# A modulation matrix applied on VectorE, ScalarE and GpSimd instead of on TensorE, in a two-layer hybrid mixer

## The chip, the cores and the metric

The kernel runs on one core of one Trainium2 chip. The metric is the device time of one execution in microseconds; the kernel before has a median of 1401.21 us in three runs. The profile is of one execution.

## The reference

Two layers are applied to a prompt (128 tokens) and to a sample (512 tokens), with a model width of 1024, and both with the same weights. A layer mixes three branches: latent attention (A), differential attention (B) and a gated linear recurrence, mLSTM (C). What matters here is the modulation at a layer's head:

```python
mod = silu(c) @ W_mod[l] + b_mod[l]            # for the sample; silu(c_ctx) for the prompt
shift, scale, gate = jnp.split(mod, 3, axis=-1)
h = rmsnorm(x, g_norm[l]) * (1 + scale) + shift
proj = h @ W_in[l]                              # 1024 x 5840, split into the branches' inputs
...                                             # branches A, B and C
y = concat([o_a * silu(z_a), o_b * silu(z_b), o_c * silu(z_c)]) @ W_out[l]
x_new = x + gate * y
```

`W_mod` is 2 x 1024 x 3072 in fp32, so a layer's `mod` is two vectors (sample and prompt) times a 1024 x 3072 matrix. All is fp32.

## The kernel before

All 640 tokens are worked on together: four tiles of 128 sample tokens and one tile of the prompt. An exact fp32 product is made of three fp32r matmuls (`mm3`, L287 to L290): each operand is split into a high part, rounded to fp32r, and the rest. For weights `load_w` (L266 to L285) does this in pieces of at most 128 x 1088 values: SyncE's queue loads a piece into one of three raw slots (L278), ScalarE casts it to the high part (L279), and VectorE, or for every third piece GpSimd, subtracts to get the low part (L282).

Work that waits on nothing but `hT`, the normalised input, is written as units that a `Feed` hands out. A dependent chain (the gates, four mLSTM heads, four heads of differential attention, the latent branch) yields a number of microseconds after each step, and `Feed.pull` emits units, portion by portion, until as much has been yielded by them. The order of the units of a layer is the string `ORDER` (L133). On top of that the framework's scheduler orders the instructions of each engine, so that a cast or a load may stand earlier than in the program. `feed.need` forces units to be finished before a chain goes on.

`W_mod` is used in units of 256 columns, 24 in all:
- Eight units (the shift and scale of layer 0) are computed at the start, when there is no other work for TensorE, unsplit. The change leaves them as they are.
- Four *gate units* per layer (`gt0` to `gt3`, `mod_gate`) make 256 columns of the residual gate each, for the same layer.
- Eight *column units* (`mod0` to `mod7`, `mod_col`), in layer 0 only, make the shift and scale of layer 1.

The last sixteen go through `mod_rows` with `pool=3`: `load_w` loads and splits two pieces of 4 x 256 columns, and sixteen matmuls with four stationary columns (the two vectors, high and low) accumulate over the 1024 rows:

```python
hv, lv = load_w([(wmod[l, :, :, c0:c0 + 256], 0, 256)], 8, 256, pool)
for k in range(8):
    T.matmul(ps[0:4, 0:256], lhsT=cst4[:, k, :], rhs=hv[k], start=(k == 0), stop=False)     # L329
    T.matmul(ps[0:4, 0:256], lhsT=cst4[:, k, :], rhs=lv[k], start=False, stop=(k == 7))     # L330
```

ScalarE copies the four rows out of PSUM (L332). A column unit then turns them into columns with two small matmuls (L344) against a constant that adds the high and the low row, and VectorE adds the bias (L347). A gate unit adds the high and low rows with one matmul (L367), adds the bias (L370) and stores two rows to `grow` in DRAM, from which `gate_tile` later loads them on all partitions for the out-projection.

Other places that the prediction's steps touch: L615 and L616 are multiply-adds of the short convolution on VectorE; L756 and L759 are products and sums of the mLSTM heads on VectorE and GpSimd; L781 is the last product of an mLSTM head; L797 is the sum of the rotary embedding on GpSimd; L990 is the first norm of the latent branch, which starts after the last head of differential attention. Tiles called `fix` and `fixr` are cut from two big ones, so many names in the trace are the same; `qt` takes one of 35 slots, `pj` one of two PSUM buffers.

Of the kernel before, what the change touches and what calls it, by code (L numbers as in the profile page):

```python
# [13 lines left out]
ALU = mybir.AluOpType  # L14
# [51 lines left out]
def parameter_columns(I):  # L66
    """Vectors of the inputs laid out as columns of 128, and the gate biases and stabilisers on their gate rows."""
# [12 lines left out]
class Feed:  # L80
    """Independent work, emitted in portions between the steps of a dependent chain."""
# [41 lines left out]
def tile_hybrid(ctx: ExitStack, tc: tile.TileContext, I: dict, O: dict):  # L123
# [8 lines left out]
    # independent work of a layer, in the order in which it fills the gaps of the dependent chains  # L132
    ORDER = ("va0 qk0 mo0 zc0 qk1 gt0 zc1 qk2 gt1 va1 mo1 zc2 "  # L133
             "gt2 qk3 zc3 lam0 dv0 gt3 dqk0 mod0 mod1 zb0 dqk1 mod2 "
             "zb1 dv1 dqk2 mod3 mod4 zb2 dqk3 mod5 c0 zb3 c1 c2 "
             "za1 za0 mod6 za2 mod7 za3")
# [3 lines left out]
    class Fixed:  # L140
        """One tile from which all that stays in its place is cut."""
# [14 lines left out]
    class Ring:  # L156
        """Slots used in turn, for tiles that live for a short stretch of the program."""
# [32 lines left out]
    # ---------------------------------------------------------------- constants and parameters  # L190
# [12 lines left out]
    # silu(cond) as stationary columns: [c_hi, ctx_hi, c_lo, ctx_lo] per k  # L203
# [5 lines left out]
    cst4 = fixr.tile([P, 8, 4])  # L209
    cv3 = cth.rearrange("p (w k) -> p k w", w=2)  # L210
# [6 lines left out]
    # half conv weights; norm gains with the half of z's silu  # L217
# [45 lines left out]
    def load_w(parts, kt, w, pool=3):  # L263
        """Streams a weight section; returns per-k views of its exact high and low parts."""
# [27 lines left out]
    # ---------------------------------------------------------------- modulation  # L292
# [4 lines left out]
    def mod_rows(l, c0, pool):  # L297
        ps = pj("modp")
        if pool is None:
            # before there is other work for the tensor engine: unsplit  # L300
# [25 lines left out]
        else:  # L326
            hv, lv = load_w([(wmod[l, :, :, c0:c0 + 256], 0, 256)], 8, 256, pool)
            for k in range(8):
                T.matmul(ps[0:4, 0:256], lhsT=cst4[:, k, :], rhs=hv[k], start=(k == 0), stop=False)  # L329
                T.matmul(ps[0:4, 0:256], lhsT=cst4[:, k, :], rhs=lv[k], start=False, stop=(k == 7))  # L330
# [4 lines left out]
    def mod_col(l, part, s, res, pool=3):  # L335
        """Columns [P, k, which] of two feature tiles of the shift or of the scale."""
# [3 lines left out]
        mr = mod_rows(l, part * 1024 + s * 256, pool)  # L340
        yield 2.5
        ps = sm("mcp")
        for i in range(2):
            T.matmul(ps[:, 2 * i:2 * i + 2], lhsT=mr[0:4, i * P:(i + 1) * P],  # L344
                     rhs=con[0:4, C_SEL:C_SEL + 2], start=True, stop=True)
# [4 lines left out]
    def mod_end(l, res, k=slice(0, 8)):  # L350
        """(1 + scale) * g and shift."""
# [11 lines left out]
    def mod_gate(l, s, pool=3):  # L363
        mr = mod_rows(l, 2048 + s * 256, pool)
        yield 2
        ps = sm("gtp")
        T.matmul(ps[0:2, 0:256], lhsT=con[0:4, C_SEL:C_SEL + 2], rhs=mr[0:4, :], start=True, stop=True)  # L367
# [860 lines left out]
    def mod_col_(part, s):  # L1228
        for _ in mod_col(0, part, s, R, None):
            pass  # L1230
# [134 lines left out]
```

## Time and profile before

| | |
|---|---|
| median of 3 runs | 1401.21 us (1399.54 to 1405.23) |
| the profiled execution | span 1399.6 us, no time listed beside it |
| TensorE busy | 1310.0 us (94%), mean granted clock 0.977 |
| VectorE, ScalarE, GpSimd busy | 842.5, 630.2, 385.5 us |
| changed units in the trace | 16, from 130.7 to 949 us |

Engines are named PE (TensorE matmuls), PEld (its weight loads), DVE (VectorE), ACT (ScalarE), POOL (GpSimd) and SP (SyncE, here only a queue of loads). An fp32 matmul shows as two records. Matmuls are pipelined: the duration of one record is longer than its distance to the next, so what a matmul occupies is read from the chain or from start to start. The chain that ended last is followed back from the last instruction to what released each step.

### The profile page before, as it was taken

The page shows a single profiled execution, that of the slowest core. Times are in us where ns is not written, and L with a number is a line of the kernel's source. Part 1 is how long each engine was busy: PE and PEld are TensorE (multiplying, and loading weights), DVE is VectorE, ACT ScalarE, POOL GpSimd, SP SyncE. Part 2 cuts the span into 40 slices and gives each one's busy share as a digit, 9 for nine tenths or more (in the row PEclk, how much of TensorE's full clock was granted, in tenths as well). Part 3 has the DMA queues.
Part 4 walks back from the last instruction along what each step waited for, and adds up shares of the span by engine and source line. Part 5 has one row for each costly group of instructions (what it writes and reads, how often), then busy time and mean ns, then how long its engine had stood idle before and what let it go on. Part 6 is the DMA issues. An engine that isn't in the chain of part 4 may idle for free.

```text
span 1399.6 us, 24039 instructions
## 1 busy us (share of the span) xinstructions
PE 1310.0 (94%) x9300; PEld 1218.9 (87%) x9300; DVE 842.5 (60%) x1786; ACT 630.2 (45%) x1333; POOL 385.5 (28%) x335
## 2 busy tenths in 40 slices
PE   8989999989899999999979899999999999899995
PEld 3789899969899999798769899998799999878984
DVE  2576757765567465854465767675655646385446
ACT  5454544433455545255365345443343445435433
POOL 0421422323223013511432213333322202161142
PEclk9999999999999999999989999999999999999998
DMA  9423323264223223531751333434521211242154
GB/s 341 116 83 101 111 84 112 85 212 136 81 83 111 61 62 113 167 109 54 238 176 31 84 112 86 117 82 129 180 84 57 74 46 63 87 138 85 54 173 150
DMA packets 164642, 156.40 MB, mean 112 GB/s; under 512 B 14193, under 2 KB 130593, under 8 KB 164529
## 3 DMA queue, kind: packets, MB, share of 16 engines
q1 hardware_dynamic: 154032, 135.92, 32.0%
q10 hardware_dynamic: 10496, 18.95, 3.6%
q8 instruction: 73, 1.20, 0.3%
q14 instruction: 41, 0.33, 0.1%
HBM read 131.38 MB, written 23.46 MB: 111 GB/s over the span
## 4 chain that ended last, share of the span: by engine, by line
PE 73%; DVE 12%; DMA 5%; ACT 4%; issue 2%; POOL 2%; SPq 1%; DVEq 0%; ACTq 0%; POOLq 0%
PE tm L288 8%; PE tm L289 8%; PE tm L290 8%; PE fm L288 6%; PE fm L290 6%; PE fm L289 6%; PE po L831 5%; PE op L288 2%; PE pT L826 2%; PE op L289 2%; PE op L290 2%; DVE fixr L282 1%; PE nd L767 1%; PE ds L921 1%; DVE ksl L816 1%
## 5 line engine op out<-in xcount | busy, mean ns | idle before, releaser
L288 PE MATMUL tm<-fixr 128*128 128x256 f32 (+2 forms) x1040 | 302.0, 291 | 12.4 <-DVE kp L816 4.8
L289 PE MATMUL tm<-fixr 128*128 128x256 f32 (+2 forms) x1040 | 299.4, 288 | 0.2 <-DVE fixr L282 0.2
L290 PE MATMUL tm<-fixr 128*128 128x256 f32 (+2 forms) x1040 | 297.0, 287 | 2.5 <-DVE fixr L427 2.2
L282 POOL TENSOR_TENSOR fixr<-fix,fixr 128x1024 fp32r<-128x1024 f32 (+4 forms) x51 | 121.4, 2380 | 385.0 <-ACT fixr L279 365.4
L279 ACT CAST fixr<-fix 128x1024 fp32r<-128x1024 f32 (+2 forms) x154 | 157.8, 1030 | 128.7 <-PE fm L289 38.4
L288 PEld LDWEIGHTS tm<-fixr 128*128 128x128 f32 x1040 | 201.0, 193 | 15.3 <-issue 4.7
L290 PEld LDWEIGHTS tm<-fixr 128*128 128x128 f32 x1040 | 200.3, 193 | 3.0 <-DVE fixr L427 2.4
L289 PEld LDWEIGHTS tm<-fixr 128*128 128x128 f32 x1040 | 201.0, 193 | 1.4 <-issue 0.9
L288 PE MATMUL fm<-fixr 128*128 128x320 f32 x640 | 201.3, 314 | 0.5 <-ACT od L940 0.5
L290 PE MATMUL fm<-fixr 128*128 128x320 f32 x640 | 199.3, 311 | 0.0
L289 PE MATMUL fm<-fixr 128*128 128x320 f32 x640 | 198.6, 310 | 0.0
L282 DVE TENSOR_TENSOR fixr<-fix,fixr 128x1024 fp32r<-128x1024 f32 (+3 forms) x103 | 141.6, 1377 | 66.8 <-ACT fixr L279 62.3
L288 PEld LDWEIGHTS fm<-fixr 128*128 128x128 f32 x640 | 120.3, 188 | 2.2 <-ACT od L940 0.8
L290 PEld LDWEIGHTS fm<-fixr 128*128 128x128 f32 x640 | 120.2, 188 | 0.9 <-issue 0.9
L289 PEld LDWEIGHTS fm<-fixr 128*128 128x128 f32 x640 | 120.4, 188 | 0.0
L539 POOL TENSOR_TENSOR xp<-xp,ytmp 128x512 f32<-128x512 f32 x60 | 79.1, 1329 | 107.7 <-DVE ytmp L538 58.4
L288 PE MATMUL op<-fixr,oTh 128*128 128x512 f32 x240 | 100.5, 419 | 2.9 <-ACT oTh L516 1.7
L289 PE MATMUL op<-fixr,oTh 128*128 128x512 f32 x240 | 96.7, 403 | 0.0
L290 PE MATMUL op<-fixr,oTl 128*128 128x512 f32 x240 | 95.0, 403 | 0.0
L929 ACT ACTIVATE P<-ds,fix 128x640 f32<-128x640 f32 (+1 forms) x80 | 56.7, 709 | 72.7 <-DVE fix L928 70.4
L927 DVE TENSOR_REDUCE fix<-ds 128x1 f32<-128x640 f32 (+1 forms) x80 | 56.8, 713 | 47.4 <-PE ds L922 31.0
L252 POOL TENSOR_TENSOR fix<-fix 128x5 f32<-128x5 f32 (+1 forms) x31 | 31.6, 1019 | 130.4 <-DVE fix L251 129.9
(325 smaller groups left out, 2722.2 us busy)
## 6 DMA issues: line engine op xcount, KB each, us to landing
fix<-in_W_in SPq DMA_DIRECT2D x56, 512.0 KB, 4.2
fix<-in_W_mod SPq DMA_DIRECT2D x35, 512.0 KB, 4.3
fix<-in_W_in SPq DMA_DIRECT2D x64, 256.0 KB, 3.3
xd<-xp ACTq DMA_DIRECT2D x60, 256.0 KB, 2.5
xp<-xd SPq DMA_DIRECT2D x50, 256.0 KB, 4.4
fix<-in_W_out SPq DMA_DIRECT2D x24, 512.0 KB, 5.0
gate<-grow SPq DMA_DIRECT2D x32, 256.0 KB, 5.0
wm<-in_W_mod SPq DMA_DIRECT2D x26, 256.0 KB, 5.9
```

The lines of the kernel that those rows point to most:

```text
L252: G.tensor_tensor(r[:, :n], a[:, :n], mhalf[:, :n], op=ALU.pow)
L279: A.copy(hv, rv)
L282: e.tensor_tensor(lv, rv, hv.bitcast(F32), op=ALU.subtract)
L288: T.matmul(ps, lhsT=wh, rhs=xh, start=start, stop=False)
L289: T.matmul(ps, lhsT=wh, rhs=xl, start=False, stop=False)
L290: T.matmul(ps, lhsT=wl, rhs=xh, start=False, stop=stop)
L539: G.tensor_tensor(xt, xt, y, op=ALU.add)
L767: T.matmul(nd[:, d, 0:129], lhsT=e[:, d], rhs=va[:, c, :], start=True, stop=(c == 4))
L826: T.transpose(ps[:, c * P:(c + 1) * P], pe[:, c * P:(c + 1) * P], idt)
L831: T.matmul(po[:, 0:P], lhsT=pt[:, c * P:(c + 1) * P], rhs=v3[:, c] if t < 4 else vp[:, hs], start=(c == 0), stop=(c == n - 1))
L927: V.tensor_reduce(sc[:, m:m + 1], pv, axis=ax, op=ALU.max, negate=True)
L929: A.activation(ev, pv, AF.Exp, scale=DIFF_SCALE, bias=sc[:, 2 + m:3 + m], accum_out=sc[:, 4 + m:5 + m])
```

## The change

The sixteen later units no longer go through the split and TensorE's sum over 1024 rows. A new unit `mod_acc` loads the same two pieces, and each partition sums its own eight values of k in fp32: for the prompt by multiply-adds on VectorE (into `a1`), for the sample by a scaled copy on ScalarE, in place in the raw slot, and an add on GpSimd (into `a0`). The scale is the partition's value of silu. What is left, the sum over 128 partitions, is done by fp32 matmuls in `mod_col` (four with a column of ones, 128 stationary columns each) and in `mod_gate` (two with a constant `two` of two columns). The `mod_acc` units are listed in `ORDER` as `ga0` to `ga3` and `ma0` to `ma7`, one or a few units ahead of the `gt` or `mod` unit that uses them, and `gt3` and `mod0` to `mod7` move a little. The loads keep their size and number. The matmuls of `mod_rows` with `pool=3`, its splits and its row copies are gone. Comments and docstrings go too, with line numbers before the first added lines unchanged.

```diff
-    ORDER = ("va0 qk0 mo0 zc0 qk1 gt0 zc1 qk2 gt1 va1 mo1 zc2 "
-             "gt2 qk3 zc3 lam0 dv0 gt3 dqk0 mod0 mod1 zb0 dqk1 mod2 "
-             "zb1 dv1 dqk2 mod3 mod4 zb2 dqk3 mod5 c0 zb3 c1 c2 "
-             "za1 za0 mod6 za2 mod7 za3")
+    ORDER = ("va0 qk0 mo0 ga0 zc0 qk1 gt0 ga1 zc1 qk2 gt1 va1 ga2 mo1 zc2 "
+             "gt2 ga3 qk3 zc3 lam0 dv0 gt3 ma0 dqk0 mod0 ma1 zb0 mod1 ma2 dqk1 mod2 ma3 "
+             "zb1 mod3 dv1 ma4 dqk2 mod4 ma5 zb2 dqk3 mod5 c0 ma6 zb3 c1 mod6 ma7 c2 "
+             "za1 za0 mod7 za2 za3")
...
+    two = fix.tile([P, 4])
+    G.memset(two, 0.0)
+    G.memset(two[:, 0:4:3], 1.0)
...
-        else:
-            hv, lv = load_w([(wmod[l, :, :, c0:c0 + 256], 0, 256)], 8, 256, pool)
-            for k in range(8):
-                T.matmul(ps[0:4, 0:256], lhsT=cst4[:, k, :], rhs=hv[k], start=(k == 0), stop=False)
-                T.matmul(ps[0:4, 0:256], lhsT=cst4[:, k, :], rhs=lv[k], start=False, stop=(k == 7))
...
+    def mod_acc(l, c0, res, key):
+        acc = qt("macc", n=512)
+        a0, a1 = acc[:, 0:256], acc[:, 256:512]
+        for k0 in (0, 4):
+            w = r_raw()[:, 0:1024].rearrange("p (k n) -> p k n", k=4)
+            nc.sync.dma_start(out=w, in_=wmod[l, :, k0:k0 + 4, c0:c0 + 256])
+            for k in range(4):
+                c_, p_ = [cth[:, x + k0 + k:x + k0 + k + 1] for x in (0, 8)]
+                if k0 + k == 0:
+                    V.tensor_scalar(a1, w[:, k], p_, None, op0=ALU.mult)
+                    A.activation(a0, w[:, k], AF.Copy, scale=c_)
+                else:
+                    V.scalar_tensor_tensor(a1, w[:, k], p_, a1, op0=ALU.mult, op1=ALU.add)
+                    A.activation(w[:, k], w[:, k], AF.Copy, scale=c_)
+                    G.tensor_tensor(a0, a0, w[:, k], op=ALU.add)
+        res[key] = acc
+        yield 0.01
...
     def mod_col(l, part, s, res):
-        mr = mod_rows(l, part * 1024 + s * 256, pool)
-        yield 2.5
+        acc = res.pop(("macc", l, 4 * part + s), None)
+        mr = mod_rows(l, part * 1024 + s * 256) if acc is None else None
         ps = sm("mcp")
         for i in range(2):
...
+                for w in range(2):
+                    T.matmul(ps[:, 2 * i + w:2 * i + w + 1], lhsT=acc[:, w * 256 + i * P:w * 256 + (i + 1) * P],
+                             rhs=con[:, C_ONE:C_ONE + 1], start=True, stop=True)
+        yield 1
...
-    def mod_gate(l, s, pool=3):
-        mr = mod_rows(l, 2048 + s * 256, pool)
-        yield 2
+    def mod_gate(l, s, res):
+        acc = res.pop(("gacc", l, s))
         ps = sm("gtp")
-        T.matmul(ps[0:2, 0:256], lhsT=con[0:4, C_SEL:C_SEL + 2], rhs=mr[0:4, :], start=True, stop=True)
+        for w in range(2):
+            T.matmul(ps[0:2, 0:256], lhsT=two[:, 2 * w:2 * w + 2], rhs=acc[:, w * 256:(w + 1) * 256],
+                     start=(w == 0), stop=(w == 1))
+        yield 0.9
```

## Rows read from the trace of the kernel before

**Rows 1.** The page: busy time of each engine, and the chain by engine.

```profile
PE 1310.0 (94%) x9300; PEld 1218.9 (87%) x9300; DVE 842.5 (60%) x1786; ACT 630.2 (45%) x1333; POOL 385.5 (28%) x335
...
PE 73%; DVE 12%; DMA 5%; ACT 4%; issue 2%; POOL 2%; SPq 1%; DVEq 0%; ACTq 0%; POOLq 0%
```

**Rows 2.** Stretches: length, busy us (instructions) of each engine, granted clock, DMA, GB/s.

```profile
core 0: us, PE busy (x) PEld busy (x) DVE busy (x) ACT busy (x) POOL busy (x), PEclk, DMA share, GB/s
71.90:271.70 199.80, 193.35 (x1482) 187.80 (x1482) 136.78 (x318) 90.73 (x201) 55.90 (x60) 0.99 0.33 99
271.70:555.20 283.50, 268.72 (x1993) 254.54 (x1993) 168.58 (x325) 133.85 (x267) 73.45 (x48) 0.98 0.34 102
...
759.80:958.30 198.50, 194.18 (x1482) 188.78 (x1480) 136.43 (x316) 90.76 (x201) 56.49 (x61) 0.98 0.34 98
```

**Rows 3.** L781 and L990, by layer: count, ns min/median/max, first and last start.

```profile
L781 DVE SCALAR_TENSOR_TENSOR hs<-mo,hs x4: 824/824/825, 140.8 to 271.7; 128x640 f32<-128x640 f32 x4
...
L990 DVE TENSOR_REDUCE fix<-jk x5: 805/810/820, 555.2 to 565.0; 128x5 f32<-128x640 f32 x5
...
L781 DVE SCALAR_TENSOR_TENSOR hs<-mo,hs x4: 825/826/2383, 829.6 to 958.3; 128x640 f32<-128x640 f32 x4
...
L990 DVE TENSOR_REDUCE fix<-jk x5: 801/820/823, 1224.7 to 1234.7; 128x5 f32<-128x640 f32 x5
```

**Rows 4.** The chain: first and last of a unit's sixteen matmuls; small matmuls.

```profile
130.96 0.12 PE modp L329
...
132.68 0.12 PE modp L330
...
136.16 0.52 PE gtp L367 x2
...
360.60 0.53 PE mcp L344 x4
```

**Rows 5.** The tile `modp`: one of the two lines, over the kernel.

```profile
L329 PE MATMUL modp<-fixr x128: 276/278/362, 130.7 to 945.7; 128*4 128x256 f32 x128
```

**Rows 6.** Groups by form on VectorE (busy us, mean ns); L756's ns min/median/max.

```profile
L282 DVE TENSOR_TENSOR fixr<-fix,fixr 128x1024 fp32r<-128x1024 f32 x94 | 129.1, 1375 | 59.8 <-ACT fixr L279 55.3 <-issue 2.3 <-PE pkd L892 1.3
...
L756 DVE TENSOR_TENSOR fix<-fix,cvt x32: 405/568/2032, 101.1 to 939.9; 128x256 f32<-128x256 f32 x32
```

**Rows 7.** Groups by form on ScalarE.

```profile
L279 ACT CAST fixr<-fix 128x1024 fp32r<-128x1024 f32 x140 | 146.0, 1048 | 112.7 <-PE fm L289 38.0 <-PE tm L290 31.6 <-DMA fix<-in_W_in 11.6
...
L755 ACT ACTIVATE fix<-mb,fix 128x128 f32<-128x128 f32 x64 | 21.1, 392 | 6.7 <-DMA mb<-msc 6.5
...
L332 ACT COPY fix<-modp 4x256 f32<-4x256 f32 x24 | 8.5, 355 | 13.8 <-PE modp L320 13.8
...
L410 ACT ACTIVATE xs<-xs,fix 128x512 f32<-128x512 f32 x10 | 6.7, 713 | 6.6 <-POOL fix L252 6.6
```

**Rows 8.** GpSimd: the subtractions by form; L797's ns min/median/max.

```profile
L282 POOL TENSOR_TENSOR fixr<-fix,fixr 128x1024 fp32r<-128x1024 f32 x46 | 112.2, 2439 | 354.2 <-ACT fixr L279 334.6 <-ACT od L940 11.7 <-ACT fix L746 5.5
...
L797 POOL TENSOR_TENSOR qk<-qk,fix x32: 724/735/1247, 265.0 to 1108.3; 128x256 f32<-128x256 f32 x32
```

**Rows 9.** Instructions of VectorE and GpSimd in order of time, 131 to 137 us.

```profile
132.38 3.15 DVE L615 SCALAR_TENSOR_TENSOR cvt<-up,fix,cvt 128x511 f32<-128x511 f32 x2
...
135.53 0.98 DVE L616 SCALAR_TENSOR_TENSOR cvt<-up,fix,cvt 128x511 f32<-128x511 f32 x2
...
132.93 2.46 POOL L282 TENSOR_TENSOR fixr<-fix,fixr 128x1024 fp32r<-128x1024 f32 x1 [17.32 <-ACT fixr L279]
```

**Rows 10.** The chain's longest steps in layer 0: start us, us, what.

```profile
150.06 2.37 DVE cvt L615 x2
...
328.45 6.90 DMA fix<-in_W_mod
...
415.21 5.46 DMA fix<-in_W_mod
```

**Rows 11.** Waits of ScalarE: total us, times, longest us.

```profile
ACT fixr L279 <- DMA fix<-in_W_in: 11.6, 6, 3.5
```

More of the change, by code (lines that the diff above doesn't have):

```diff
@@ L295, in tile_hybrid, with mod_rows @@
     first = [None]
-    def mod_rows(l, c0, pool):
+    def mod_rows(l, c0):
         ps = pj("modp")
-        if pool is None:
+        if True:
             for k in range(0, 8, 4):
@@ L333, in mod_rows, with mod_col @@
         return mr
-    def mod_col(l, part, s, res, pool=3):
+    def mod_acc(l, c0, res, key):
[15 more added lines that the diff above has]
+        yield 0.01
+    def mod_col(l, part, s, res):
         if ("mc", l) not in res:
@@ L339, in mod_col @@
         mc = res["mc", l]
-        mr = mod_rows(l, part * 1024 + s * 256, pool)
-        yield 2.5
+        acc = res.pop(("macc", l, 4 * part + s), None)
+        mr = mod_rows(l, part * 1024 + s * 256) if acc is None else None
         ps = sm("mcp")
         for i in range(2):
-            T.matmul(ps[:, 2 * i:2 * i + 2], lhsT=mr[0:4, i * P:(i + 1) * P],
-                     rhs=con[0:4, C_SEL:C_SEL + 2], start=True, stop=True)
+            if acc is None:
+                T.matmul(ps[:, 2 * i:2 * i + 2], lhsT=mr[0:4, i * P:(i + 1) * P],
+                         rhs=con[0:4, C_SEL:C_SEL + 2], start=True, stop=True)
+            else:
+                for w in range(2):
+                    T.matmul(ps[:, 2 * i + w:2 * i + w + 1], lhsT=acc[:, w * 256 + i * P:w * 256 + (i + 1) * P],
+                             rhs=con[:, C_ONE:C_ONE + 1], start=True, stop=True)
+        yield 1
         b0 = R_BM + 24 * l + 8 * part + 2 * s
@@ L1228, in mod_col_ @@
     def mod_col_(part, s):
-        for _ in mod_col(0, part, s, R, None):
+        for _ in mod_col(0, part, s, R):
             pass
@@ L1261, in tile_hybrid @@
             "va": lambda i: sec_va(l, hT, i, R), "qk": lambda i: sec_qk(l, hT, i, R), "mo": lambda i: sec_mo(l, hT, i, R),
-            "zc": lambda i: z_sec(l, hT, "zc", OFF["zc"], R, i), "gt": lambda i: mod_gate(l, i),
+            "zc": lambda i: z_sec(l, hT, "zc", OFF["zc"], R, i), "gt": lambda i: mod_gate(l, i, R), "ga": lambda i: mod_acc(l, 2048 + i * 256, R, ("gacc", l, i)),
+            "ma": lambda i: mod_acc(l + 1, i * 256, R, ("macc", l + 1, i)),
             "lam": lambda i: lambdas(l), "dv": lambda i: sec_dv(l, hT, i, R), "dqk": lambda i: sec_dqk(l, hT, i, R),
@@ L1267, in tile_hybrid @@
         order = [(u[:-1], int(u[-1])) for u in ORDER.split()]
-        order = [u for u in order if u[0] != "mod" or l + 1 < DEPTH]
+        order = [u for u in order if u[0] not in ("mod", "ma") or l + 1 < DEPTH]
         add = feed.add
@@ L1289, in tile_hybrid @@
             feed.along(diff_head(l, h, R, feed))
-        feed.need("opc", *[u for u in order if u[0] != "mod"])
+        feed.need("opc", *[u for u in order if u[0] not in ("mod", "ma")])
         add("opb", out_proj(l, 1, range(4), R, "ob", 4 * l + 1))
```

## The prediction

> **What bounds the kernel now.** I read the profile from the coarse to the fine. The page says that TensorE is busy for 94% of the span and that 73% of the chain that ended last runs on it, with VectorE at 12%, ScalarE at 4% and GpSimd at 2% [rows 1]. An average hides stages, so the table by stretch comes next. In the two stretches of layer 0 that hold all its changed units TensorE is busy for 193.4 of 199.8 and 268.7 of 283.5 us, in layer 1's gate stretch for 194.2 of 198.5, at a granted clock of 0.98 to 0.99; VectorE has 59 to 69% there, GpSimd 26 to 28% [rows 2]. So there the work on TensorE itself sets the time, and a piece of it that disappears should show.
>
> The trace holds a natural experiment on that. Both layers run the same code, but only layer 0 has the eight column units (mod0 to mod7). From the last head's L781 to the first norm of the latent branch (L990) layer 0 takes 555.2 - 271.7 = 283.5 us and layer 1 takes 1224.7 - 958.3 = 266.4 us [rows 3]: 17.1 us for eight units, 2.14 us each. In the stretch before it, with four gate units in both layers, the two differ by 1.3 us only (199.8 against 198.5) [rows 2], which is about how well such a comparison can be trusted.
>
> What one unit occupies is read from the chain: its sixteen matmuls run from 130.96 to 132.80 us, 1.84 us [rows 4]. A column unit adds four records of 0.53 us together [rows 4], so 2.37 us, and eight of them 19.0 us. The contrast found 17.1 us: **0.90 of the work taken off TensorE comes back as time**.
>
> **The change, part by part.**
>
> *TensorE.* The 128 matmuls of L329 and as many of L330 go [rows 5]: 16 units x 1.84 = 29.4 us. The small matmuls grow. A column unit had two fp32 matmuls of two records each; now it has four, on 128 partitions, so eight records with the same 128 stationary columns. Nearest rows: 0.133 us a record of mcp, 0.115 of modp [rows 4]; bounds 0.92 and 1.06 us. I take 1.06, since as many columns are loaded: +0.53 x 8 = 4.2 us. A gate unit had one fp32 matmul of 256 columns, two records in 0.52 us [rows 4]; now two matmuls: +0.52 x 8 = 4.2 us. Net 29.4 - 8.4 = 21.0 us off TensorE, and at 0.90 of it **18.9 us gained**.
>
> *VectorE.* 32 split pieces go. By the code one piece in three is subtracted on GpSimd, so about 21 subtractions leave VectorE at 1.375 us and 11 leave GpSimd at 2.439 us [rows 6, 8]: -28.9 us and -26.8 us. In come 128 multiply-adds of 128x256, both inputs in SBUF. The nearest row is L756, the same shape with two SBUF inputs and with GpSimd adding beside it: 0.405 us at the least, 0.568 in the median [rows 6]. That makes +52 to +73, net +23 to +44 us. I take +44, since here too GpSimd adds right behind.
>
> *ScalarE.* Off: 32 casts at 1.048 and 16 copies at 0.355 us, 39.2 us [rows 7]. On: 128 scaled copies of 256 columns. That shape from SBUF is not in the trace; 128 columns take 0.392 and 512 take 0.713 us [rows 7], which bounds it, and a straight line between gives 0.50. 64 - 39 = +25 us.
>
> *GpSimd.* On: 112 adds of 128x256. L797 has that shape: 0.735 us in the median, 1.247 at most [rows 8]. +82 - 27 = +55 us, +113 at the upper bound.
>
> *What the additions cost.* None of their results is wanted soon: an accumulator is used one or more units after it is begun. What they cost is the queue in front of others. The price goes from 0 (all in idle time: VectorE is idle for 63 of the 199.8 us and for 115 of the 283.5 [rows 2]) to the share of each engine's work that already lies on the chain: VectorE's 12% of 1399.6 is 168 of 842 us busy, 0.20; ScalarE 56 of 630, 0.09; GpSimd 28 of 385, 0.07 [rows 1]. That upper end is 44 x 0.20 + 25 x 0.09 + 55 x 0.07 = 15 us. The new work can wait, the old on the chain can't, and no row lies nearer to either end, so I take the middle, **7.5 us lost**.
>
> One row speaks against a small price. At 132.38 us a pair of multiply-adds of L615 (two SBUF inputs) takes 3.15 us, where the pair of L616 takes 0.98; GpSimd runs a 2.46 us subtraction from 132.93 to 135.39, and VectorE is through at 135.53 [rows 9]. It stood still until GpSimd had ended.
> The Trainium skill says this outright (SBUF — State Buffer, section "Who interferes with whom"): a VectorE instruction with two SBUF inputs and a GpSimd instruction that reads SBUF exclude each other, and the later one waits for the whole of the other; the row agrees. By the rule alone a unit's multiply-adds and adds can't overlap at all.
> From the rows, eight multiply-adds of 0.405 and seven adds of 0.735 in turn are 8.4 us of both engines per unit, against 8 x 0.568 = 4.5 us in my sum: 16 x 3.9 = 62 us more of VectorE's time, standing still, 12 us at its 0.20. It is rival C below.
>
> *Loads and queues.* The 32 loads stay the same on SyncE's queue, one or two units earlier in the list, but each holds one of three raw slots longer. Before: cast 1.05, then 1.4 us on VectorE or 2.4 on GpSimd, 2.8 us in the mean. After: until the fourth add, 0.57 + 0.50 + 4 x 0.735 = 4.0 us, or 5.7 if multiply-adds and adds take turns; 38 to 93 us more for 32 loads. Behind a load that waits for its slot stand the next W_in pieces and the out-projection's residual tiles. What hides it: W_in kept ScalarE waiting for only 11.6 us in all [rows 11]. Two W_mod loads are themselves on the chain, 6.90 and 5.46 us [rows 10]; afterwards ScalarE, VectorE and GpSimd all have an instruction behind such a load, but no matmul stands directly behind it. I set these against each other at nothing; the bounds are -12 (both waits gone) and +19 (half of the 38).
>
> *The rest.* A gate unit now yields between its matmuls and its row, so ScalarE's queue issues the bias load and the store to `grow` one portion later, and the gate tiles are loaded from `grow`. All four gate units are forced out before the out-projection is queued, so I count nothing; without that cover it is a portion of 0.9 us for the last one. An accumulator takes one of 35 slots for a unit or two, and a unit no longer needs one of the two `pj` buffers: nothing, and bounded by the same 0.9 us a unit either way. The constant `two` costs two memsets at the start.
>
> **Sum.** 1399.6 - 18.9 + 7.5 = 1388.2 us of span. The profiled execution lists no time beside its span; the median of the runs is 1.6 us above it, so 1390 us on that scale, 0.8% faster.
>
> **Rivals.**
>
> A. *Nothing given back*: the additions find idle time, all 21.0 us come back, and the two W_mod waits may go too. 1399.6 + 1.6 - 21 = 1380, down to 1368; case A is 1368 to 1382. For it: VectorE is idle for 31 to 41% of these stretches. Against it: a queue in order finds no hole exactly when it is needed.
>
> B. *Cancelled by the loads.* Raw slots are held 1.2 us longer or more, 32 times; a W_in piece comes late, its cast too, and TensorE waits. If 10 to 19 us of the 38 us or more reach the chain, the additions costing nothing or their 7.5 us, the time is 1392 to 1409. For it: the W_mod loads on the chain [rows 10]. Against it: the small W_in wait [rows 11].
>
> C. *Slower: VectorE held by GpSimd's adds.* Place: the mLSTM and attention steps between two matmuls, where VectorE has two-input work on the chain (at 150.06 us the chain spends 2.37 us in a pair of L615 [rows 10]). Price: 55 us more GpSimd time; if all of it delayed the chain, 55 - 18.9 = 36 us slower. It breaks even where a third of it reaches the chain and decides (over 7 us slower) at 26 of 55, 47%. Half of it gives 1399.6 + 27.5 - 18.9 + 1.6 = 1410 us. The Trainium skill's exclusion (SBUF — State Buffer, above) is the rule behind it. Against it: adds of 0.735 us replace subtractions of 2.439 us, so that a single stop is shorter, and only 0.07 of GpSimd's work lies on the chain today.
>
> D. *Nothing is taken off the path*: the freed TensorE time is waited out, since the matmuls behind are not ready. Then only the additions count: 1401 to 1416 with 0 to 15 us of them. The layer contrast speaks against it.
>
> **How the numbers follow.** 0.5% is 7 us, about what a measurement can tell from no change. The forecast (1382 to 1397, from a price of 0 to 15 us) has a chance of 0.48, A 0.11, B 0.18, C 0.16, D 0.07. Faster by over 0.5% (under 1394.2): A, 0.42 of the forecast, 0.05 of B: 0.58. Slower by over 0.5% (over 1408.2): 0.15 of C and 0.03 of D: 0.18. The rest, 0.24, is the same. The likeliest case's own range is 1382 to 1397; the range that leaves out two in ten is 1376 to 1410: it cuts off the far end of A (0.05) and most of C and D's end (0.15).
>
> **What would show it.** Right: TensorE's busy time falls by about 20 us; the stretch from the last L781 to L990 of layer 0 shrinks by up to 17.1 x (2.37 - 1.06) / 2.37 = 9.5 us, each layer's stretch with the gate units by up to 4 x 1.32 x 0.90 = 4.8; GpSimd gains about 55 us, VectorE up to 44, ScalarE 25. Wrong: multiply-adds with a mean near 1 us, adds above 1 us, VectorE's or GpSimd's share of the chain up by several points, TensorE's idle time growing by 20 us (C); more waits of ScalarE's casts for W_in (B); the same stretches with less TensorE work in them (D). What would make the prediction wrong first is the price of the additions, which no row of before gives.

## The result, and the profile after

The changed kernel takes 1492.7 us (median of 4 runs, 1492.2 to 1494.9) beside 1400.9 us of the kernel before on the same chip: ratio 1.065, 95% interval 1.063 to 1.067. It is 6.5% slower. The forecast was 1390 us, and the range ended at 1410.

The page of the changed kernel, busy time by engine and the chain by engine (compare [rows 1]):

```profile
PE 1324.8 (89%) x9092; PEld 1228.2 (82%) x9092; DVE 870.6 (58%) x1893; ACT 655.8 (44%) x1413; POOL 450.8 (30%) x438
...
PE 61%; DVE 13%; DMA 8%; ACT 6%; issue 6%; POOL 5%; SPq 1%; ACTq 0%; DVEq 0%; POOLq 0%
```

TensorE runs 208 matmuls fewer than before and is busy for 14.8 us more. Its share of the chain falls from 73 to 61%; DMA, ScalarE, GpSimd and "issue" (an engine waits for nothing that the profile shows) all rise. TensorE has less to do and more of the chain runs elsewhere.

The stretches between the landmarks of [rows 3], which are now L807 and L1016: to the last L807 of layer 0, to L1016, to the last L807 of layer 1, to L1016 of layer 1.

```profile
core 0: us, PE busy (x) PEld busy (x) DVE busy (x) ACT busy (x) POOL busy (x), PEclk, DMA share, GB/s
0.00:301.60 301.60, 268.14 (x1837) 237.46 (x1838) 180.16 (x427) 137.05 (x304) 99.41 (x119) 0.95 0.40 121
301.60:633.60 332.00, 274.82 (x1871) 261.24 (x1870) 177.90 (x360) 140.10 (x293) 93.55 (x86) 0.89 0.30 89
633.60:1055.70 422.10, 382.21 (x2618) 356.06 (x2618) 259.74 (x585) 192.75 (x419) 144.66 (x148) 0.96 0.37 110
1055.70:1317.90 262.20, 248.37 (x1820) 237.97 (x1819) 147.69 (x304) 115.61 (x242) 56.69 (x41) 0.99 0.29 86
```

Before, the same four took 271.7, 283.5, 403.1 and 266.4 us [rows 3]. So 29.9, 48.5 and 19.0 us are lost in the three stretches in which W_mod pieces are loaded and summed, and nothing in the fourth, which has none. (The stretches don't hold equal work: the first has 1837 matmuls, before 1836, though its four gate units have 56 fewer, so matmuls of other units have moved into it.) The granted clock falls with them: 0.89 in the second, 0.98 before [rows 2].

What waits, in total us, times, longest. The last row is SyncE's queue:

```profile
ACT fixr L282 <- DMA fix<-in_W_in: 111.4, 43, 8.3
...
ACT fix L348 <- DVE macc L347: 44.2, 63, 3.7
...
SPq L281 <- POOL macc L349: 196.6, 28, 35.7
```

ScalarE's casts of W_in waited 11.6 us before, 6 times [rows 11]; now 111.4 us, 43 times. The last row is new: the issues of weight loads (L281) stand for 196.6 us, up to 35.7 at once, until an *add of an accumulator* (L349) has ended. The add frees a raw slot. The total alone isn't a loss. Before, the same queue stood even longer for the subtractions that free its slots, and W_in was hardly ever late:

```profile
SPq L278 <- DVE fixr L282: 270.9, 46, 16.3
SPq L278 <- POOL fixr L282: 208.9, 36, 24.4
```

So the row says where to look, and the loss has to be seen in a single case.

One such case in full. SyncE's issues from 376 to 440 us (L340 loads a W_mod piece, L281 a piece of W_in; rows are start, us, queue, line):

```profile
378.79 0.37 SPq L340 DMA_DIRECT2D fix<-in_W_mod  x1
...
406.36 0.37 SPq L340 DMA_DIRECT2D fix<-in_W_mod  x1
...
415.08 0.37 SPq L340 DMA_DIRECT2D fix<-in_W_mod  x1
...
435.80 0.93 SPq L281 DMA_DIRECT2D fix<-in_W_in  x2
```

At 415 us the three raw slots hold three W_mod pieces (issued at 378.79, 406.36, 415.08), and no W_in piece can be loaded. Next the chain from there on:

```profile
429.86 0.12 PE tm L292
429.98 1.13 PE po L857 x10
...
432.34 0.40 ACT macc L345
...
434.99 0.79 POOL macc L349
...
435.80 0.38 SPq L281
...
436.22 3.33 DMA fix<-in_W_in
...
440.76 2.36 POOL fixr L285
...
443.17 0.58 PE tm L292
443.75 0.21 PE tm L293
```

and VectorE's first product of that piece:

```profile
429.65 0.34 DVE L344 TENSOR_SCALAR macc<-fix 128x256 f32<-128x256 f32 x1
```

The first piece was issued at 378.79 (a W_mod load lands 3.7 us after its issue in the median); its products begin on VectorE at 429.65 and on ScalarE at 432.34, the last of its adds (three for a unit's first piece) ends at 435.78, and 0.02 us later SyncE issues the W_in load. It lands, is cast and subtracted, and TensorE goes on at 443.17. One piece held its slot for 57 us, and for some 47 of them it lay there untouched. The stretches around it:

```profile
415.00:430.00 15.00, 14.82 (x121) 14.60 (x121) 9.93 (x27) 5.22 (x11) 1.56 (x1) 1.00 0.17 49
430.00:441.00 11.00, 2.64 (x21) 2.36 (x21) 5.54 (x9) 5.88 (x12) 5.66 (x8) 0.74 0.24 61
441.00:456.00 15.00, 13.37 (x87) 13.07 (x88) 6.23 (x17) 3.76 (x8) 4.88 (x4) 0.74 0.38 114
```

TensorE is busy for 2.64 of 11 us, and when it starts again a matmul of `tm` takes 0.21 us where it took 0.12 ahead of the stop: it runs for a while at the lower of its two levels, 1.2 GHz and 2.4 GHz. So a stop is paid twice. The Trainium skill (TensorE: Matmul & The Clock Gate, section "What's actually happening") says that the throttled clock is the default and that activity releases it; the 0.74 behind the stop agrees.

### The profile page after: what moved, and what is told of

Its sections match the earlier page's. It is cut to its first block, busy times and chain, and to the rows that moved or that the text cites. A ratio compares the mean times of both kernels' runs of the same rounds, so it can differ in the third digit from the quotient of the medians.

```text
span 1493.1 us, 23970 instructions
## 1 busy us (share of the span) xinstructions
PE 1324.8 (89%) x9092; PEld 1228.2 (82%) x9092; DVE 870.6 (58%) x1893; ACT 655.8 (44%) x1413; POOL 450.8 (30%) x438
## 4 chain that ended last, share of the span: by engine, by line
PE 61%; DVE 13%; DMA 8%; ACT 6%; issue 6%; POOL 5%; SPq 1%; ACTq 0%; DVEq 0%; POOLq 0%
PE tm L292 7%; PE tm L291 6%; PE tm L293 6%; PE po L857 4%; DMA fix<-in_W_in 4%; PE fm L293 4%; PE fm L291 4%; PE fm L292 4%; PE op L291 3%; PE op L293 2%; PE op L292 2%; PE pT L852 2%; POOL macc L349 2%; DVE fixr L285 2%; ACT fixr L282 1%
## 5 line engine op out<-in xcount | busy, mean ns | idle before, releaser
L291 PE MATMUL tm<-fixr 128*128 128x256 f32 (+2 forms) x1040 | 308.1, 298 | 33.8 <-ACT fixr L282 32.7
L292 PE MATMUL tm<-fixr 128*128 128x256 f32 (+2 forms) x1040 | 305.6, 294 | 9.7 <-DVE fixr L285 5.4
L293 PE MATMUL tm<-fixr 128*128 128x256 f32 (+2 forms) x1040 | 303.8, 293 | 2.8 <-DVE fixr L453 2.2
L291 PEld LDWEIGHTS tm<-fixr 128*128 128x128 f32 x1040 | 207.2, 200 | 38.1 <-ACT fixr L282 33.9
L291 PE MATMUL fm<-fixr 128*128 128x320 f32 x640 | 204.9, 320 | 17.7 <-ACT fixr L282 17.6
L292 PEld LDWEIGHTS tm<-fixr 128*128 128x128 f32 x1040 | 207.7, 200 | 12.0 <-DVE fixr L285 6.8
L293 PEld LDWEIGHTS tm<-fixr 128*128 128x128 f32 x1040 | 206.6, 199 | 3.6 <-DVE fixr L453 2.4
L293 PE MATMUL fm<-fixr 128*128 128x320 f32 x640 | 200.9, 316 | 5.0 <-POOL fixr L285 3.6
L292 PE MATMUL fm<-fixr 128*128 128x320 f32 x640 | 201.5, 315 | 0.0
L282 ACT CAST fixr<-fix 128x1024 fp32r<-128x1024 f32 (+5 forms) x122 | 124.8, 1025 | 162.7 <-DMA fix<-in_W_in 111.4
L285 DVE TENSOR_TENSOR fixr<-fix,fixr 128x1024 fp32r<-128x1024 f32 (+5 forms) x82 | 105.9, 1294 | 100.9 <-ACT fixr L282 100.1
L285 POOL TENSOR_TENSOR fixr<-fix,fixr 128x1024 fp32r<-128x1024 f32 (+3 forms) x40 | 94.8, 2371 | 220.6 <-ACT fixr L282 220.6
L291 PEld LDWEIGHTS fm<-fixr 128*128 128x128 f32 x640 | 123.4, 193 | 19.7 <-ACT fixr L282 18.8
L349 POOL TENSOR_TENSOR macc<-macc,fix 128x256 f32<-128x256 f32 x112 | 92.7, 827 | 125.5 <-ACT fix L348 113.6
L293 PEld LDWEIGHTS fm<-fixr 128*128 128x128 f32 x640 | 122.6, 192 | 7.3 <-POOL fixr L285 4.4
L292 PEld LDWEIGHTS fm<-fixr 128*128 128x128 f32 x640 | 123.2, 193 | 0.4 <-issue 0.4
```

The lines of the kernel that those rows point to most:

```text
L282: A.copy(hv, rv)
L285: e.tensor_tensor(lv, rv, hv.bitcast(F32), op=ALU.subtract)
L291: T.matmul(ps, lhsT=wh, rhs=xh, start=start, stop=False)
L292: T.matmul(ps, lhsT=wh, rhs=xl, start=False, stop=False)
L293: T.matmul(ps, lhsT=wl, rhs=xh, start=False, stop=stop)
L349: G.tensor_tensor(a0, a0, w[:, k], op=ALU.add)
```

## The experiments

Two kinds of theory stood at the start. *Slots* (S in the expectations): W_mod pieces hold the three shared raw slots too long; S1 says that the sums take long, S2 that they begin long after the piece has landed. *Queues and order* (L, A and O there): the new instructions, or the new order and portions of the units, delay what stands behind them. All kernels, with the ratio to the kernel before that ran on the same chip (e2, e3 and e4 have two runs, e8 three, e5, e7, e10, e11 and e15 four, the others five to twelve):

| run | kernel | us | ratio (95%) |
|---|---|---|---|
| e1 | changed, W_mod in 2 raw slots of its own | 1399.3 | 0.998 (0.997 to 0.999) |
| e2 | changed, one k of four summed | 1431.9 | 1.020 (1.018 to 1.023) |
| e3 | before, two raw slots | 1412.7 | 1.007 (1.005 to 1.009) |
| e4 | changed, copies not in place | 1481.2 | 1.056 (1.053 to 1.058) |
| e5 | changed, own accumulator slots | 1431.3 | 1.022 (1.019 to 1.025) |
| e6 | own raw slots and own accumulators | 1407.8 | 1.004 (1.002 to 1.005) |
| e7 | own raw slots, one k of four summed | 1385.4 | 0.988 (0.986 to 0.990) |
| e8 | own raw slots, copies not in place | 1410.1 | 1.006 (1.004 to 1.008) |
| e9 | before, own raw slots | 1408.8 | 1.004 (1.003 to 1.005) |
| e10 | own raw slots, prompt's sums only | 1383.3 | 0.986 (0.985 to 0.988) |
| e11 | own raw slots, sample's sums only | 1384.8 | 0.987 (0.986 to 0.988) |
| e12 | own raw slots, all sums on VectorE | 1400.7 | 0.998 (0.996 to 0.999) |
| e13 | e1, sums issued step by step | 1398.4 | 0.997 (0.995 to 0.998) |
| e14 | e12, sums issued step by step | 1407.3 | 1.003 (1.002 to 1.004) |
| e15 | changed, four shared raw slots | 1422.7 | 1.013 (1.011 to 1.015) |
| e16 | before, the new order and portions | 1407.9 | 1.004 (1.002 to 1.006) |
| e17 | own raw slots, all sums on ScalarE and GpSimd | 1397.1 | 0.997 (0.995 to 0.998) |
| e18 | e12, every second subtraction on GpSimd | 1406.3 | 1.004 (1.002 to 1.006) |

**e1, own slots.**

```diff
+    r_mod = Ring(2, 1024, fix)
...
-            w = r_raw()[:, 0:1024].rearrange("p (k n) -> p k n", k=4)
+            w = r_mod().rearrange("p (k n) -> p k n", k=4)
```

> The changed kernel, with the W_mod pieces of the accumulating units loaded into two slots of their own, so that W_in keeps the three raw slots for itself. Theory S (W_in loads wait for a raw slot that an accumulation still holds): ScalarE's casts wait for W_in for under 30 us in all instead of 111 us, and most of the 92 us comes back: 1385 to 1415 us. Theory L (VectorE and GpSimd exclude each other and VectorE's steps come late): the same adds run, so 1475 to 1495 us. Theory O (the new order of units and the smaller yields put TensorE's work in a worse order): the order is the same, 1475 to 1495 us. Theory A (casts stand behind scaled copies that wait for VectorE, 44 us in 63 waits): the copies are the same, 1465 to 1495 us.

1399.3 us: (1.0646 - 0.998) x 1401 = 93 us come back, the whole loss. ScalarE's wait for W_in falls from 111.4 to 3.7 us:

```profile
ACT fixr L283 <- DMA fix<-in_W_in: 3.7, 3, 2.3
```

Order, arithmetic and engines are those of the changed kernel; only the place of the pieces differs. The slots are the loss.

**e2, one k of four**, so that the other three of each piece are not summed; shared slots.

```diff
-            for k in range(4):
+            for k in range(1):
...
-                    A.activation(w[:, k], w[:, k], AF.Copy, scale=c_)
-                    G.tensor_tensor(a0, a0, w[:, k], op=ALU.add)
```

> The changed kernel with seven eighths of the accumulation left out: of each loaded piece of four k only the first is used, so that each piece has one multiply on VectorE, one scaled copy on ScalarE or none, and no add on GpSimd; its modulation is not the reference's. Loads, order of units and TensorE's small matmuls stay. S: the slots are free soon after landing, 1380 to 1400 us. L: no adds, 1380 to 1400 us. A: 1380 to 1400 us. O: the order remains, over 1450 us. It also bounds what the freed TensorE time is worth: by the prediction's own step 21.0 us x 0.90 against before, 1382 us.

1431.9 us, which none of the theories had expected. With hardly any arithmetic 31 us of loss remain, and ScalarE still waits 108.6 us for W_in. With own slots the same kernel takes 1385.4 us (e7), so sharing costs 46 us here, half of the 93, although there is almost nothing to sum: a piece keeps its slot also while nothing is done with it.

**e3, the kernel before with two slots** (`RAW` 3 to 2).

> The kernel before with two raw slots instead of three, nothing else. S: losing one slot of three is enough to make W_in late; 1450 to 1550 us, with ScalarE's casts waiting for W_in for over 80 us. L, O and A: nothing of theirs is in it, 1400 to 1415 us.

1412.7 us: one slot gone for good costs the kernel before only 0.7%, where *Slots* had expected 1450 us or more. So the loss of the changed kernel isn't that of one slot; at moments all three are held, as at 415 us above.

**e4, copies not in place**: ScalarE's product goes to a tile `et("mt")` and GpSimd adds that, so that a copy needn't wait until VectorE has read the piece (44.2 us of waits above).

```diff
-                    A.activation(w[:, k], w[:, k], AF.Copy, scale=c_)
-                    G.tensor_tensor(a0, a0, w[:, k], op=ALU.add)
+                    t = et("mt")
+                    A.activation(t, w[:, k], AF.Copy, scale=c_)
+                    G.tensor_tensor(a0, a0, t, op=ALU.add)
```

> The changed kernel, with ScalarE's scaled copy written to one of the eight 256-column work tiles instead of in place, so that a raw slot is free when VectorE and ScalarE have read it and no longer has to wait for GpSimd's adds, and the copy needn't wait for VectorE's read. S: the hold gets shorter by the adds' tail, some 2 to 4 us of 7 each; a third to two thirds of the loss comes back, 1430 to 1465 us. A: the 44 us of waits vanish, 1445 to 1465 us. L and O: 1480 to 1495 us.

1481.2 us, 12 us of 92, less than S and A had expected: this wait is a small part, and W_in is still waited for, 95.0 us. With own slots the same edit makes it slower (e8), so it isn't the in-place copy that costs there.

**e5, own accumulators; raw slots shared.** In the changed kernel an accumulator is one of the 35 `qt` slots, which are handed out in the program's order.

```diff
+    r_acc = Ring(3, 512, fix)
...
-        acc = qt("macc", n=512)
+        acc = r_acc()
```

> The changed kernel with the accumulators in a ring of three 512-column tiles of their own instead of in the 35 shared slots; the W_mod pieces are again loaded into the three shared raw slots. Theory S1 (a raw slot is held long because the sums take long: three engines in turn): the sums take as long as before, so little comes back, 1450 to 1495 us. Theory S2 (the slot is held because the sums begin late: an accumulator gets its shared slot only in the order of the program, 30 to 60 us after its piece has landed): the sums begin within some 10 us of the landing, ScalarE's casts wait for W_in for under 40 us, and the time is 1385 to 1420 us.

1431.3 us: 61 us come back by this edit alone, somewhat less than S2 had expected and far more than S1. In the changed kernel the first unit is loaded from 57.8 us and summed from 103 us on; these two rows are its loads and its adds, from SyncE's and GpSimd's order in time:

```profile
57.76 2.60 SPq L340 DMA_DIRECT2D fix<-in_W_mod  x2
```

```profile
106.86 6.10 POOL L349 TENSOR_TENSOR macc<-macc,fix 128x256 f32<-128x256 f32 x7 [3.64 <-issue]
```

The same in e5, SyncE's issues (lines are one higher) and VectorE's sums:

```profile
56.77 2.59 SPq L341 DMA_DIRECT2D fix<-in_W_mod  x2
```

```profile
60.39 0.35 DVE L345 TENSOR_SCALAR fix<-fix 128x256 f32<-128x256 f32 x1 [1.26 <-DMA fix<-in_W_mod]
60.78 1.53 DVE L348 SCALAR_TENSOR_TENSOR fix<-fix 128x256 f32<-128x256 f32 x3
...
64.03 2.59 DVE L348 SCALAR_TENSOR_TENSOR fix<-fix 128x256 f32<-128x256 f32 x3
```

The sums now start when the piece lands. So what held the piece was the wait for the *accumulator's* slot, while the load had gone ahead as soon as a raw slot was free. What e5 still loses may be its waits, now for W_mod itself (no run takes these away alone):

```profile
ACT fix L346 <- DMA fix<-in_W_mod: 23.7, 11, 4.9
DVE fix L345 <- DMA fix<-in_W_mod: 18.0, 11, 4.7
ACT fixr L283 <- DMA fix<-in_W_in: 10.2, 5, 4.2
```

ScalarE and VectorE stand in order behind a piece that hasn't landed. W_in is down to 10.2 us.

**e6, both; e7, own raw slots with one k of four; e8, own raw slots with the copy aside.** e6 has both edits of e1 and e5 (two slots each), e7 those of e1 and e2, e8 those of e1 and e4.

> Own slots for the W_mod pieces (two) and own accumulators (two). S1 and S2 both: like the run with own slots alone, 1390 to 1402 us. If what is missing there against the forecast gain of 19 us lies in sums that begin late, 1380 to 1390 us; if it is the price of the additions themselves (7.5 us forecast, 15 at the upper end), it stays at 1392 to 1402 us.

> Own slots, and of each loaded piece only one k of four is used (one multiply on VectorE, at most one scaled copy on ScalarE, no add on GpSimd): seven eighths of the arithmetic are left out and the modulation is not the reference's. This is what the work taken off TensorE is worth when nearly nothing is added elsewhere. By the forecast's 21.0 us x 0.90: 1380 to 1386 us. If the removed matmuls are worth less, over 1390 us. The difference to the run with own slots is the price of the additions; forecast 7.5 us, 0 to 15.

> Own slots, and ScalarE's scaled copies written to the 256-column work tiles instead of in place, so that ScalarE needn't wait for VectorE's read of the same columns. Theory A (the copies that wait for VectorE hold up ScalarE's queue): 3 to 8 us faster than own slots alone, 1391 to 1396 us. Otherwise within 3 us of it, or slower, since the eight work tiles turn faster.

e6, 1407.8 us, more than expected: with own raw slots an early start of the sums is no gain, a loss of 8 us rather. e7, 1385.4 us, is the changed kernel without nearly all its additions and without its slot loss: 0.0119 x 1401 = 16.7 us faster than before. That is the gain of the smaller work on TensorE, forecast at 18.9. And e1 against e7 is the price of the additions: (0.998 - 0.988) x 1401 = 14 us, forecast at 7.5. e8, 1410.1 us: slower than e1, with 19.6 us of ScalarE's waits for W_mod.

**e9, the kernel before with own raw slots**: its W_mod pieces too go through a ring of two, nothing else.

> The kernel before, with W_mod's later pieces in two raw slots of their own; nothing else changed. If own slots help only because the new arithmetic holds a slot for long, the kernel before doesn't gain from them: 1397 to 1404 us, ratio 0.997 to 1.002. Rival: own slots are worth something by themselves (the two W_mod loads of 6.9 and 5.5 us on the chain of before, the 11.6 us of W_in waits): 1386 to 1395 us; then so much of what was read as TensorE's gain from the kernel with own slots and one of four k (1385.4 us) belongs to the slots.

1408.8 us, slightly slower. Own slots are worth nothing to the old arithmetic, so the gain of e7 doesn't come from the slots (set against e9 it is 22 us, 0.0160 x 1401).

**e10 to e12, which additions cost.** e10 leaves out the sample's copies and adds but the first copy, e11 the prompt's multiply-adds but the first product; e12 makes both sums on VectorE:

```diff
-                    A.activation(w[:, k], w[:, k], AF.Copy, scale=c_)
-                    G.tensor_tensor(a0, a0, w[:, k], op=ALU.add)
+                    V.scalar_tensor_tensor(a0, w[:, k], c_, a0, op0=ALU.mult, op1=ALU.add)
```

> Own slots, VectorE's sums (the prompt's half) whole; ScalarE's scaled copies and GpSimd's adds left out but for the first copy, so that the sample's sums are not made. The price of the additions with own slots was 14 us. If it comes from VectorE and GpSimd standing in each other's way, the multiply-adds go back from a mean of 0.72 us to about 0.4 and nearly all comes back: 1384 to 1389 us. If each engine's added work costs by itself, VectorE's half stays: 1390 to 1396 us.

> Own slots, ScalarE's copies and GpSimd's adds whole (the sample's half); VectorE's multiply-adds left out but for the first product, so that the prompt's sums are not made. If the two engines' meeting is the price, nearly all comes back here too, 1384 to 1390 us, less what the adds hold other work of VectorE. If VectorE's own work is the price, the same 1384 to 1388 us, and the run with the prompt's half alone is at 1396 to 1399. If ScalarE and GpSimd are the price, 1394 to 1399 us here.

> Own slots, both sums as multiply-adds on VectorE, no GpSimd add and one ScalarE copy a unit; the whole result is made. VectorE gets 240 multiply-adds; at 0.4 us, the least of the nearest row, they are 96 us against 81 us for 112 at the mean of 0.72. If VectorE and GpSimd in each other's way are the price: 1384 to 1392 us, faster than the kernel before by about 1%. If VectorE's queue is the price: 1400 to 1412 us.

1383.3 and 1384.8 us: *either half is free*. 1400.7 us: both on one engine cost as much as on two. e10 and e11 were what the theory of two engines in each other's way expected, but e12 pays the same without a single add on GpSimd, so the meeting of the sums' own multiply-adds and adds isn't needed for the price. (What it is worth in e1 alone no run tells.) The exclusion that the Trainium skill states (SBUF — State Buffer, "Who interferes with whom"), of a VectorE instruction with two SBUF inputs and a GpSimd instruction that reads SBUF, shows in the multiply-adds, 0.48 us in the median of e10 and 0.56 of e1.

**e13 and e14, step by step.** A unit's eight steps go into a list, and each portion of filler work issues one, in place of all eight at once; what is left is issued before the result is read.

```diff
+        if self.side:
+            self.side.pop(0)()
...
+                def add(k=k, k0=k0, w=w):
...
+                side.append(add)
```

> Own slots, all sums; a unit's eight steps (multiply-add, copy, add) are issued one by one, one with each portion of filler work, in place of all at once. Either half of the sums alone cost nothing, both together 14 us. If the price is the lump of eight steps in front of the steps of the chain on VectorE, it falls and the kernel beats both: 1384 to 1393 us. If it is the total of VectorE's work, or the meeting of multiply-add and add one at a time, nothing changes: 1397 to 1403 us.

> Own slots, both sums on VectorE (1400.7 us when issued at once), issued one step at a time. Lump theory: 1384 to 1393 us. Total-work theory: 1397 to 1403 us. If this one gains and the kernel with GpSimd's adds does not, what is left there is the meeting of the two engines.

1398.4 and 1407.3 us: the lump of eight isn't the price.

**e15 and e16, the slots and the order directly.** e15 is the changed kernel with `RAW` 4; the 1635 us in its expectation are summed over the 32 pieces, each from its issue to the end of the last instruction that reads it. e16 is the kernel before with the mod units at their new places and with yields of 1 and 0.9 us.

> The changed kernel with four raw slots shared by all, in place of three. In the changed kernel the W_mod pieces hold slots for 1635 us in all between 57 and about 970 us, 1.8 of the three slots in the mean. If that is the loss, four slots leave some 2.2 for the other weights and the time lies between the kernel before with two slots (1412.7) and the changed one (1492.7), at 1415 to 1445 us, and ScalarE's waits for W_in fall from 111 to 20 to 60 us. If the order of the work is the cause: 1480 to 1495 us.

> The kernel before with the new order of its units (the mod units moved as in the change) and the new, shorter portions of 1 and 0.9 us; the arithmetic is that of before. If order and portions are no part of the loss: 1395 to 1408 us. If they are a part of it: more, up to 1490 us for all of it.

1422.7 us, as expected: one more shared slot gives back 70 of 92 us. ScalarE's waits for W_in are 72.9 us, more than expected, so the waits' sum isn't proportional to the time. e16, 1407.9 us: order and portions cost 0.4% (0.2 to 0.6) of the 6.5.

**e17 and e18, work taken off VectorE.** e17 makes the prompt's sums as ScalarE copies and GpSimd adds too; e18 is e12 with `pool=2`.

> Own slots, both sums as ScalarE copies and GpSimd adds (240 copies, 224 adds), VectorE with one product a unit. In the runs with own slots VectorE's busy time goes with the price: 816 to 860 us with none, 889 and 897 with 14 to 15 us. If VectorE's total is what costs, this one (VectorE at about 820 to 840) is at 1384 to 1392 us, faster than both kernels by about 1%. If any further work on top of one half costs, whatever the engine: 1397 to 1410 us.

> Own slots, both sums on VectorE, and every second instead of every third weight piece subtracted on GpSimd: about 18 subtractions of 1.38 us leave VectorE (some 25 us, to about 872) and GpSimd gets them at 2.44 us. If VectorE's total is what costs: 1385 to 1395 us, from 1400.7. If the subtractions on GpSimd come late for TensorE or hold VectorE: 1400 to 1415 us.

1397.1 and 1406.3 us: neither gains as VectorE's total would have it. In e17 VectorE is busy for 823.5 us, nearly as little as in e7 (818.1), and yet the price is there. The theory of VectorE's total falls by this run. e18 doesn't bear on it, since its VectorE total didn't fall: 896.1 us, 897.1 in e12. 18 of the large subtractions left, but the others took 1.448 us in the mean in place of 1.371, and the multiply-adds took longer too.

**Where the 14 us are.** e7 has TensorE busy for 1282.8 of 1383.3 us, e1 for 1293.2 of 1395.7 with the same 9092 matmuls. Of 12.4 us between the spans 10.4 are matmuls that take longer and 2.0 idle time. The places can be found. In e1 VectorE from 354 us on:

```profile
355.92 0.91 DVE L348 SCALAR_TENSOR_TENSOR macc<-fix,macc 128x256 f32<-128x256 f32 x1
...
357.27 2.04 DVE L348 SCALAR_TENSOR_TENSOR macc<-fix,macc 128x256 f32<-128x256 f32 x4
359.59 3.33 DVE L843 TENSOR_TENSOR ksl<-pkd,ksh 64x640 fp32r<-64x640 f32 x4 [0.28 <-ACT kp L840]
362.93 1.19 DVE L843 TENSOR_TENSOR kp<-pkd,kp 64x128 fp32r<-64x128 f32 x4
364.13 0.49 DVE L873 COPY vv<-tm 128x128 f32<-128x128 f32 x2
```

Five multiply-adds of an accumulator, then the splits of a key, then the copies of `vv`, which empty a PSUM buffer. The multiply-adds aren't what made the splits late: ahead of them VectorE waited 0.28 us for ScalarE's cast `kp`, and on ScalarE three products of the sums (354.01 to 355.33 us) stand ahead of these casts. TensorE waits for `vv`, and its stretches around that are (the same columns as above):

```profile
PE tm L292 <- DVE vv L873: 3.2, 1, 3.2
```

```profile
350.00:362.00 12.00, 11.57 (x87) 11.34 (x86) 11.18 (x16) 10.06 (x20) 5.49 (x6) 1.00 0.39 104
362.00:366.00 4.00, 1.23 (x8) 1.26 (x9) 3.89 (x10) 1.21 (x4) 2.02 (x3) 0.94 0.58 164
366.00:370.00 4.00, 4.00 (x21) 4.00 (x20) 0.67 (x3) 1.10 (x2) 0.00 (x0) 0.50 0.74 227
370.00:374.00 4.00, 4.00 (x27) 4.00 (x26) 1.99 (x5) 0.00 (x0) 1.17 (x1) 0.71 0.02 6
```

A stop of 3.2 us, and behind it the granted clock is 0.50 and 0.71 for 4 us each, which loses, by an estimate from these clocks, 4 x 0.50 + 4 x 0.29 = 3.2 us more: 6.4 us. The whole stretch between the landmarks is 272.8 us in e1 and 265.2 in e7, 7.6 us apart. e13 and e17 have the same wait for `vv` (3.2 and 3.6 us); e12, e14 and e18 have one of 3.2 to 3.4 us there, of the unit's own matmul for its sum (`mcp` for `macc`). Of e7, e10 and e11 none has a TensorE wait over 1.1 us at that place, and e10 is at a granted clock of 1.00 throughout:

```profile
352.00:364.00 12.00, 11.54 (x93) 11.21 (x91) 10.25 (x21) 5.71 (x12) 1.14 (x1) 1.00 0.54 155
364.00:376.00 12.00, 11.11 (x91) 11.05 (x91) 8.58 (x19) 5.55 (x10) 1.74 (x3) 1.00 0.03 10
```

A second stop stands at the head of the same stretch. In e1:

```profile
PE oT L540 <- DVE hs L534: 3.7, 1, 3.7
```

```profile
280.91 2.95 DVE L534 TENSOR_TENSOR hs<-hs,fix 128x640 f32<-128x640 f32 x1 [1.10 <-POOL fix L256]
280.84 2.34 POOL L286 TENSOR_TENSOR fixr<-fix,fixr 128x1024 fp32r<-128x1024 f32 x1
```

```profile
278.00:282.00 4.00, 2.21 (x11) 1.46 (x9) 2.46 (x5) 1.83 (x3) 2.29 (x2) 1.00 1.00 302
282.00:286.00 4.00, 2.08 (x11) 2.09 (x11) 2.98 (x3) 0.00 (x0) 1.18 (x1) 0.70 0.44 124
286.00:290.00 4.00, 4.00 (x21) 3.31 (x20) 1.81 (x3) 2.50 (x4) 1.58 (x1) 0.88 0.65 216
```

The norm's product L534 takes 2.95 us beside a weight piece's subtraction on GpSimd; in e7 the same product takes 0.80 and is nearly through when that subtraction begins. TensorE stands for 3.7 us and loses about 2.08 x 0.30 + 4 x 0.12 = 1.1 us more by the clock (an estimate as above): 4.8 us. The same wait of `oT` for `hs` is 3.7 us in e6, 5.3 in e8, 3.7 in e12, 3.6 in e13, 4.3 in e14, 2.9 in e17 and 1.7 in e18. In e7, e10, e11 and the kernel before there is none at that place. (In e17 and e18 the granted clock behind it stays at 1.00.) In e1 the two stops make 11.2 us. From the start to the end of the stretch e1 takes 277.0 + 272.8 and e7 273.6 + 265.2 us, 11.0 apart. (The 3.4 us of the first part are no loss of their own: e1 has 26 more matmuls in it and 27 fewer in the second.)

So nearly all of the price in e1 is two stops and the slower matmuls behind them. That this is why either half is free and both are not was read from the traces, not tried by moving these two steps.

## Why the prediction was wrong

The step that failed is "Loads and queues": "I set these against each other at nothing; the bounds are -12 [...] and +19". It measured 93 us (the changed kernel against e1). The hold of a slot was counted from the landing to the fourth add, 4.0 to 5.7 us, as if the sums began when the piece lands. In the trace a piece holds its slot for 51 us in the mean (1635 us over 32 pieces, from the issue of the load), and most of that is waiting for its sums (47 of 57 us in the case above). The prediction itself had the two halves of this: the loads would be issued early and "An accumulator takes one of 35 slots for a unit or two", costed at nothing. It didn't put them together: a load needs only a raw slot, the sums need the accumulator too and wait for it, and the piece sits in between. Before, a piece left its raw slot as soon as it was cast and subtracted, into rings of five. The cover that it named, the small W_in wait of 11.6 us [rows 11], was true of the old hold alone.

By its own steps:

- *TensorE*: right in its total, and partly by luck. Forecast 18.9 us, measured 16.7 (e7 against before). It is made up otherwise than forecast: in e7 TensorE's busy time falls by 27.2 us, not 21.0, and its idle time grows by 10.9 (from 89.6 to 100.5), and the two errors nearly cancel. The kernel before has a stop of its own at 366 us, a wait of 3.0 us for `sz` (L496) with a granted clock of 0.50 behind it, which e7 doesn't have; no row of the forecast counts it. Small matmuls: 1.06 us for eight of `mcp` forecast, 0.79 us in the chain of the changed kernel at 388.14 us.
- *The work on the other engines*: near. VectorE +28 us (forecast 23 to 44; +47 in e1), ScalarE +26 (25), GpSimd +65 (55). The tile's rows, ns min/median/max:

```profile
L347 DVE SCALAR_TENSOR_TENSOR macc<-fix,macc x112: 462/622/1037, 105.7 to 992.3; 128x256 f32<-128x256 f32 x112
L349 POOL TENSOR_TENSOR macc<-macc,fix x112: 722/786/1598, 106.9 to 993.5; 128x256 f32<-128x256 f32 x112
```

- *What the additions cost*: forecast 7.5 us, with an upper bound of 15; measured 14 with own slots. The bound held; the way didn't. The price isn't a share of each engine's added work: half of the work costs nothing, on whichever engine, and nearly all of the whole, in e1, is two stops with their clock.
- *The rest* (order, portions): counted at nothing; e16 has 0.4% (0.2 to 0.6), about what the text gave as the limit of a measurement.
- *Rival B* had the mechanism, W_in late behind held slots, and a price of 10 to 19 us from 38 to 93 us of holding. *Rival C* (VectorE held by GpSimd) isn't the 93 us: e1 has the same adds and none of that loss. *Rival D* fails by e7.
- Of the signs that it gave, B's came: "more waits of ScalarE's casts for W_in (B)" is what the trace shows. The sign of being right didn't: TensorE's busy time rose by 14.8 us where it should have fallen by about 20. TensorE's idle time grew too, from 89.6 to 168.3 us, but for B's reason and not for C's.

None of the kernels here that do the whole work beats the kernel before by 0.5%: the best, e13 and e17, are 0.3% faster.

## What to carry to other kernels

A buffer's hold runs from the issue of the load to its last reader, and the last reader waits for everything *it* needs, its output slot too. Ask of each load in a shared ring what its consumer waits for; if that is pinned to a place in the program and the load isn't, the load will run ahead and sit in the ring. Give such pieces a ring of their own (or an output of their own), and then cost what is left by whether TensorE stops for it, not by a share of engine time.

## What was not expected of the hardware

- The same matmul takes 0.21 us behind a stop of TensorE where it takes 0.12 ahead of it; after 11 us with 2.64 busy, at a granted clock of 0.74 for the next 15. Of the 109.8 us between the spans of the changed kernel and e7, which run the same 9092 matmuls, 67.8 are idle time of TensorE and 42.0 are matmuls that take longer (1324.8 against 1282.8 us busy).
- A stop as short as 3.2 us is followed by 8 us at 0.50 and 0.71 (e1, 366 to 374 us), and costs as much again.
